# Two float32r products instead of one float32 product for the four gate rows

## The chip, the cores and the metric

The kernel runs on one core of a Trainium2 chip. The core has five engines that work side by side and are tied together by semaphores: TensorE (PE, matrix products; PEld is its weight load), VectorE (DVE), ScalarE (ACT), GpSimd (POOL) and SyncE (SP, which here only issues DMAs). The metric is the device time of one launch in microseconds. The kernel before has a median of 1128.47 us over 3 runs (1128.34 to 1129.39).

## The reference, cut to what matters

One decoder block over 1024 tokens of width 1024, all in float32. A vector of modulations is made from the conditioning vector `c`, and its six parts of 1024 numbers shift, scale and gate the two sub-layers:

```python
cond = jax.nn.silu(c)
mod = cond @ w_ada + b_ada
sh_a, sc_a, gt_a, sh_m, sc_m, gt_m = split(mod, 6)
h = rms_norm(x, g_attn_pre) * (1 + sc_a) + sh_a
...                                    # projection, attention in two kinds of heads, output projection
x = x + gt_a * rms_norm(y, g_attn_post)
h = rms_norm(x, g_mlp_pre) * (1 + sc_m) + sh_m
y = square(relu(h @ w_up)) @ w_down
x = x + gt_m * rms_norm(y, g_mlp_post)
```

The change is about the sums of `cond @ w_ada` for the two gates, `gt_a` and `gt_m`. Each gate has 1024 columns and is made in two groups of 512, so there are four such sums.

## The kernel before, in words

**The modulations.** `w_ada` has 1024 rows; each of the 128 partitions holds 8 of them. The columns behind the first 2048 are worked in eight groups `g` of 512 columns, each in four pieces. `ada_piece` (L1002) loads a piece into a tile `wa_st`, multiplies it by the partition's `cond` and adds it to an accumulator `ada_acc` of 128x512: on POOL for the first 24 pieces (groups 0 to 5, during projection and attention), on DVE for the last 8 (groups 6 and 7, during the MLP). After the fourth piece the 128 partitions have to be summed. For groups 2 to 5 this gives columns, in eight small products. For groups 0, 1, 6 and 7, the gates, the sum is wanted as a row repeated on all partitions: one float32 product with a 128x128 matrix of ones, `f_fin` at L1037, into a PSUM tile `ada_ps`. It stands in the profile as two matmul instructions for each product. The step is planned as `fin`:

```python
T.matmul(b[0][:, :512], ones[:], ada.acc[:, :512], start=True, stop=True)                       # L1037
ef = pe_op("fin", 0.86 if row else 0.45, f_fin, [e], takes=[(r_ps, 1)], gives=[(r_acc or r_adacc, 1)])   # L1041
```

Behind it `f_gl` (L1048, L1049) loads the bias and the gain into a tile `gate_st`, `f_g1` (L1054) adds the PSUM tile to it on DVE and so frees the bank, `f_g2` (L1060, L1062) multiplies, and the row goes to DRAM (`gate_d`), to be read much later as `gate_a` and `gate_m`.

**The rest.** After a start with the loading of `x` and the first modulations, the input projection (`pj`, L875 to L878) runs on PE interleaved with attention: scores `s_ps`, transposes `pt_ps`, probabilities times values `o_ps`, and transposes of values `pv` (L846). Then come the output projection (`y_ps`) and the MLP (`mlp_ps`, L1991 to L1993), where each 512x512 block product is split by sums of blocks into seven products. All large products are made of float32r parts: an operand is cast to a high part on ACT, its low part is made by a subtraction on DVE (or POOL), and three products of parts are added in PSUM. The weights of the projection are split in this way at L549 (ACT) and L554 (DVE or POOL), the probabilities at L1258 and L1262.

**Buffers.** `stage()` (L454) gives a tile of 4 KB a partition: up to the end of the projection one of five (`r_stg`), shared by `wa_st`, `gate_st`, the rotated queries and keys `hl` and the output weights `wo_st` and `wo_hi`; in the MLP one of four that are counted out of a larger pool. `ada_acc` is one buffer (`r_adacc`) in the first part and one of the `stage()` tiles in the MLP. The PSUM bank `x` (`r_x`) is used by `ada_ps`, by `pv`, by every second `o_ps` and, in the MLP, by block products.

**The order.** No engine chooses its order at run time. A planner in the program (`Sched`) goes through all steps before anything is emitted: each step has an engine, an estimated duration, the steps it depends on, buffers that it takes and gives, and a priority. It keeps a clock for each engine, always takes the step that can start earliest by its estimates, and writes the instructions in that order. PE's steps are in named streams, and `prefer()` (L2153) says which stream goes first; `fin` is preferred only 1.0 us after its inputs are due (`SURE`, L143). Loads of priority 15 to 24 are put off by 3 us (`SLACK`, L145). On the chip each engine runs its written order and waits by semaphores. So a step with other durations, or other buffers, can change the order of all steps that are planned after it.

Of the kernel before, what the change touches and what calls it, by code (L numbers as in the profile page):

```python
# [10 lines left out]
F32 = mybir.dt.float32  # L11
F32R = mybir.dt.float32r
# [3 lines left out]
ALU = mybir.AluOpType  # L16
# [3 lines left out]
P = 128  # L20
# [157 lines left out]
class Sched:  # L178
# [21 lines left out]
    def op(self, eng, dur, emit, deps=(), **kw):  # L200

        o = self.step(dur, emit, deps, **kw)
        o.alts = None
        if isinstance(eng, str):
            self.queue[eng].append(o)
        else:
            o.alts = dict(zip(eng, zip(dur, emit)))
            for e in eng:
                self.queue[e].append(o)
        return o.ev  # L210

    def pe_op(self, stream, dur, emit, deps=(), **kw):
        o = self.step(dur, emit, deps, **kw)
        o.alts = None
        self.pe.setdefault(stream, []).append(o)
        return o.ev
# [116 lines left out]
def t_as(n):  # L333
    return 0.2 + 0.00083 * n


def t_dv(n):
    return 0.066 + 0.00104 * n
# [19 lines left out]
def hybrid_block(ctx: ExitStack, tc: tile.TileContext, x, positions, w_ada, b_ada, g_attn_post, w_in, w_out,  # L358
# [3 lines left out]
    V, A, G, T = nc.vector, nc.scalar, nc.gpsimd, nc.tensor  # L362
# [3 lines left out]
    op, pe_op = sc.op, sc.pe_op  # L366
# [9 lines left out]
    const = ctx.enter_context(tc.tile_pool(name="const", bufs=1))  # L376
# [7 lines left out]
    def ring_r(name):  # L384

        return ph2.right.tile([P, 1024], F32, name=name, tag="right")
# [7 lines left out]
    r_stg, r_w, r_wst, r_hl = Res(5), Res(WR), Res(WS), Res(0)  # L394
# [10 lines left out]
    inv_f = head[:, CW_F:CW_F + 8]  # L405
    scl = [head[:, CW_SCL + i:CW_SCL + i + 1] for i in range(2)]
    ones = const.tile([P, P], F32, name="ones")
    nhalf = const.tile([P, KC], F32, name="nhalf")
    cond = const.tile([P, KC], F32, name="cond")
    bb = const.tile([P, KC, 2], F32, name="bb")  # L410
# [43 lines left out]
    def stage(name):  # L454
        if st.stgp is None:
            return ring_r(name)
        return st.stgp.tile([P, 1024], F32, name=name, tag="stg")

    def load(emit, nbytes, deps=(), takes=(), prio=5, gives=(), after=None, n=1):
        return op("SP", nbytes / (345e3 if prio > -500 else 370e3), emit, deps, takes=takes, prio=prio, gives=gives, after=after, n=n)  # L460
# [30 lines left out]
    r_wa, r_acc = Res(NWA), Res(2)  # L491
# [84 lines left out]
    def f_init():  # L576
        V.memset(ones[:], 1.0)
        V.tensor_copy(ones_r[:].rearrange("p (a b) -> p a b", b=P), ones[:].unsqueeze(1).to_broadcast([P, 4, P]))
        V.memset(nhalf[:], -0.5)
    e_init = op("DVE", 0.4, f_init, prio=0)  # L580
    e = op("ACT", 0.1, lambda: A.activation(cond[:], c_raw, AF.Exp, scale=-1.0), [e_c], prio=0)

# [31 lines left out]
    e = op("DVE", 4.2, f_turns, [e_pos, e_c], prio=1)  # L614

    def f_sin():
# [5 lines left out]
                prio=1)  # L622
# [89 lines left out]
    def tables(groups, place, r_place, r_bank, bank, deps):  # L712
# [30 lines left out]
       prio=8)  # L743
# [253 lines left out]
    ada = Tok()  # L997
    ada.i, ada.acc, ada.e, ada.raw, ada.gate = 0, None, Ev(0.0), {}, {}
    e_mod = {}
    r_adacc = Res(1)  # L1000

    def ada_piece(i, eng, accp, psum, r_ps, r_acc=None):  # L1002
        g, jp = divmod(i, 4)
        col = 2 * D + g * 512

        def f_load():
            ada.raw[i] = stage("wa_st")
            nc.sync.dma_start(ada.raw[i][:].rearrange("p (j n) -> p j n", j=2),
                              ada_view[:, 2 * jp:2 * jp + 2, col:col + 512])
        el = load(f_load, 524288, takes=[(r_stg, 1)], prio=20)  # L1010

        def f_acc():
            wa = ada.raw.pop(i)[:].rearrange("p (j n) -> p j n", j=2)
            if jp == 0:
                ada.acc = accp()
            for j in range(2):
                cj = cond[:, 2 * jp + j:2 * jp + j + 1]
                if jp == 0 and j == 0:
                    eng.tensor_scalar(ada.acc[:, :512], wa[:, 0], cj, 1.0, ALU.mult, ALU.mult)
                elif eng is V:  # L1020
                    V.scalar_tensor_tensor(ada.acc[:, :512], wa[:, j], cj, ada.acc[:, :512], ALU.mult, ALU.add)
                else:
                    G.tensor_scalar(wa[:, j], wa[:, j], cj, 1.0, ALU.mult, ALU.mult)
                    G.tensor_tensor(ada.acc[:, :512], ada.acc[:, :512], wa[:, j], ALU.add)  # L1024
        e = op("DVE" if eng is V else "POOL", 1.2 if eng is V else 4.1, f_acc,
               [el, ada.e], takes=[(r_acc or r_adacc, 1)] if jp == 0 else [], gives=[(r_stg, 1)], prio=9)
        ada.e = e
        if jp < 3:
            return
        b = []  # L1030
        row = g in (0, 1, 6, 7)
        n0 = (g % 2) * 512

        def f_fin():
            b.append(psum())
            if row:
                T.matmul(b[0][:, :512], ones[:], ada.acc[:, :512], start=True, stop=True)  # L1037
            else:
                for k in range(4):
                    T.matmul(b[0][:, k:k + 1], ada.acc[:, k * P:(k + 1) * P], ones[:, 0:1], start=True, stop=True)  # L1040
        ef = pe_op("fin", 0.86 if row else 0.45, f_fin, [e], takes=[(r_ps, 1)],  # L1041
                   gives=[(r_acc or r_adacc, 1)])
        if row:
            gate, gp = (gate_d[0], g_attn_post) if g < 2 else (gate_d[1], g_mlp_post)

            def f_gl():
                ada.gate[g] = t = stage("gate_st")
                nc.sync.dma_start(t[:, 0:512], b_ada[0:1, col:col + 512].to_broadcast([P, 512]))  # L1048
                nc.sync.dma_start(t[:, 512:1024], gp[0:1, n0:n0 + 512].to_broadcast([P, 512]))  # L1049
            eg = load(f_gl, 524288, [e], takes=[(r_stg, 1)], prio=19)  # L1050

            def f_g1():
                t = ada.gate[g]
                V.tensor_tensor(t[:, 0:512], b[0][:, :512], t[:, 0:512], ALU.add)  # L1054
            e1 = op("DVE", t_dv(512), f_g1, [ef, eg], gives=[(r_ps, 1)], prio=4)

            def f_g2():
                t = ada.gate[g]
                if g < 2:
                    V.tensor_tensor(t[:, 0:512], t[:, 0:512], t[:, 512:1024], ALU.mult)  # L1060
                else:
                    V.scalar_tensor_tensor(t[:, 0:512], t[:, 0:512], D ** 0.5, t[:, 512:1024], ALU.mult, ALU.mult)  # L1062
            e2 = op("DVE", t_dv(512), f_g2, [e1], prio=4)
            e_mod[g] = load(lambda: nc.sync.dma_start(gate[:, n0:n0 + 512], ada.gate[g][:, 0:512]), 262144, [e2],
                            gives=[(r_stg, 1)], prio=18)
        else:
            k0 = n0 // P

            def f_c():
                if g < 4:  # L1070
                    V.tensor_tensor(s_m[:, k0:k0 + 4], b[0][:, 0:4], cols[:, 40 + k0:44 + k0], ALU.add)
                else:
                    V.tensor_tensor(g_m[:, k0:k0 + 4], b[0][:, 0:4], b1m[:, k0:k0 + 4], ALU.add)
                    V.tensor_tensor(g_m[:, k0:k0 + 4], g_m[:, k0:k0 + 4], cols[:, 16 + k0:20 + k0], ALU.mult)
            e_mod[g] = op("DVE", 0.15, f_c, [ef], gives=[(r_ps, 1)], prio=4)

    def feed_ada():
        if st.d > 1.0 + ada.i * 4.1 / NADA and ada.i < NADA:
            ada_piece(ada.i, G, lambda: adp.tile([P, 512], F32, name="ada_acc", tag="ada_acc", bufs=1), lambda: px.tile([P, 512], F32, name="ada_ps", tag="x"), r_x)
            ada.i += 1  # L1080
        return ada.i == NADA
# [1052 lines left out]
    def feed_ada2():  # L2134
        if ada.i < 32:
            if ada.i >= NADA and ml.begun > 8 + 2 * (ada.i - NADA):
                ada_piece(ada.i, V, lambda: stage("ada_acc"),
                          lambda: px.tile([P, 512], F32, name="ada_ps", tag="x"), r_x, r_stg)
                ada.i += 1
            return False  # L2140

        def f_gate():
            ml.gate = ring_r("gate_m")
            nc.sync.dma_start(ml.gate[:], gate_d[1][:])
        ml.e_gate = load(f_gate, 524288, [e_mod[6], e_mod[7]], takes=[(r_h2, 1)], prio=17)
        return True
# [32 lines left out]
```

## Time and profile before

| what | value |
|---|---|
| median of 3 runs | 1128.47 us (1128.34 to 1129.39) |
| time of the profiled execution | 1129.15 us |
| its span, first to last instruction | 1127.1 us |
| PE busy in the span | 1107.0 us |
| DVE, ACT, POOL busy | 817.2, 636.8, 255.4 us |
| mean granted TensorE clock | 0.996 |
| starts of the four gate products (L1037) | 117.8, 158.4, 663.9 and 813.7 us |

The span is the profiled time less 2.05 us of start and end. Busy time of PE includes the pipeline of a matmul, so two that overlap count once; the distance between starts is the better price of one.

### The profile page before, as it was taken

The page shows a single profiled execution, that of the slowest core. Times are in us where ns is not written, and L with a number is a line of the kernel's source. Part 1 is how long each engine was busy: PE and PEld are TensorE (multiplying, and loading weights), DVE is VectorE, ACT ScalarE, POOL GpSimd, SP SyncE. Part 2 cuts the span into 40 slices and gives each one's busy share as a digit, 9 for nine tenths or more (in the row PEclk, how much of TensorE's full clock was granted, in tenths as well). Part 3 has the DMA queues.
Part 4 walks back from the last instruction along what each step waited for, and adds up shares of the span by engine and source line. Part 5 has one row for each costly group of instructions (what it writes and reads, how often), then busy time and mean ns, then how long its engine had stood idle before and what let it go on. Part 6 is the DMA issues. An engine that isn't in the chain of part 4 may idle for free.

```text
span 1127.1 us, 15613 instructions
## 1 busy us (share of the span) xinstructions
PE 1107.0 (98%) x5417; PEld 920.9 (82%) x5417; DVE 817.2 (73%) x1379; ACT 636.8 (56%) x1111; POOL 255.4 (23%) x336
## 2 busy tenths in 40 slices
PE   8999999999999999999999999999999999999997
PEld 6788888888888788788888888888888888888885
DVE  7968767666686576579889564798743996537998
ACT  8769767455665576677575334653145632246542
POOL 2447777567751131110000000000000000000003
PEclk9999999999999999999999999999999999999999
DMA  9564665554513642565861268711578112584104
GB/s 349 177 215 132 196 225 194 178 173 153 197 43 146 232 147 80 203 235 213 321 242 38 76 233 310 249 52 42 186 252 318 38 56 95 199 307 165 38 19 150
DMA packets 93215, 193.69 MB, mean 172 GB/s; under 512 B 8656, under 2 KB 31312, under 8 KB 93136
## 3 DMA queue, kind: packets, MB, share of 16 engines
q1 hardware_dynamic: 93136, 192.69, 49.2%
q8 instruction: 43, 0.70, 0.3%
q14 instruction: 36, 0.29, 0.1%
HBM read 141.28 MB, written 32.51 MB: 154 GB/s over the span
## 4 chain that ended last, share of the span: by engine, by line
PE 77%; ACT 7%; DVE 6%; DMA 3%; issue 3%; POOL 3%; SPq 1%; POOLq 0%; DVEq 0%; ACTq 0%
PE mlp_ps L1992 17%; PE mlp_ps L1991 17%; PE mlp_ps L1993 17%; PE pj L875 3%; PE pj L878 3%; PE pj L876 3%; PE s_ps L1139 3%; PE o_ps L1274 2%; PE y_ps L1545 2%; PE y_ps L1547 2%; PE y_ps L1546 1%; PE pt_ps L1244 1%; ACT p_sb L1214 1%; PE pt_ps L1247 1%; DMA o_sb<-o_dram 1%
## 5 line engine op out<-in xcount | busy, mean ns | idle before, releaser
L1991 PE MATMUL mlp_ps<-hw 128*128 128x512 f32 x896 | 349.6, 390 | 0.0
L1993 PE MATMUL mlp_ps<-hw 128*128 128x512 f32 x896 | 348.6, 389 | 0.0
L1992 PE MATMUL mlp_ps<-hw 128*128 128x512 f32 x896 | 348.6, 389 | 0.0
L1991 PEld LDWEIGHTS mlp_ps<-hw 128*128 128x128 f32 x896 | 168.2, 188 | 35.8 <-issue 0.5
L1992 PEld LDWEIGHTS mlp_ps<-hw 128*128 128x128 f32 x896 | 168.2, 188 | 35.2 <-issue 0.5
L1993 PEld LDWEIGHTS mlp_ps<-hw 128*128 128x128 f32 x896 | 168.2, 188 | 34.9
L1755 DVE TENSOR_TENSOR hw<-w,hw 128x1024 fp32r<-128x1024 f32 x96 | 114.6, 1219 | 95.2 <-ACT hw L1748 93.2
L1748 ACT CAST hw<-w 128x1024 fp32r<-128x1024 f32 x96 | 97.6, 1048 | 130.0 <-PE mlp_ps L1993 97.5
L2101 POOL TENSOR_TENSOR st<-st,nhalf 128x1 f32<-128x1 f32 x8 | 8.0, 1011 | 592.6 <-DVE st L2099 592.6
L875 PE MATMUL pj<-hw,w_hl 128*128 128x512 f32 x240 | 101.8, 424 | 0.0
L878 PE MATMUL pj<-hw,w_hl 128*128 128x512 f32 x240 | 94.7, 394 | 0.0
L876 PE MATMUL pj<-hw,w_hl 128*128 128x512 f32 x240 | 94.3, 393 | 0.0
L1262 DVE TENSOR_TENSOR ph<-pt_ps,ph 128x512 fp32r<-128x512 f32 (+1 forms) x110 | 68.2, 647 | 24.7 <-ACT ph L1258 24.5
L1748 ACT CAST hw<-u 128x1024 fp32r<-128x1024 f32 x48 | 48.7, 1052 | 64.6 <-PE mlp_ps L1993 64.6
L1258 ACT CAST ph<-pt_ps 128x512 fp32r<-128x512 f32 (+1 forms) x110 | 57.3, 557 | 24.1 <-PE pt_ps L1247 20.3
L1755 DVE TENSOR_TENSOR hw<-u,hw 128x1024 fp32r<-128x1024 f32 x48 | 57.0, 1218 | 18.2 <-ACT hw L1748 18.2
L1165 ACT ACTIVATE p_sb<-p_sb,mn 128x128 f32<-128x128 f32 (+3 forms) x64 | 49.7, 777 | 35.1 <-DVE mn L1158 32.2
L1170 POOL TENSOR_SCALAR p_sb<-p_sb,den 128x128 f32<-128x128 f32 (+3 forms) x64 | 49.0, 771 | 74.1 <-DVE den L1168 66.3
L2049 DVE TENSOR_TENSOR yacc<-yacc,mlp_ps 128x512 f32<-128x512 f32 x96 | 62.1, 681 | 3.3 <-PE mlp_ps L1993 3.3
L1024 POOL TENSOR_TENSOR ada_acc<-ada_acc,wa_st 128x512 f32<-128x512 f32 x42 | 55.8, 1328 | 3.5
L1545 PE MATMUL y_ps<-hw,oh 128*128 128x512 f32 x128 | 52.6, 411 | 0.9 <-DVE mn L1158 0.4
L878 PEld LDWEIGHTS pj<-hw,w_hl 128*128 128x128 f32 x240 | 45.1, 188 | 10.3
(207 smaller groups left out, 1994.1 us busy)
## 6 DMA issues: line engine op xcount, KB each, us to landing
hw<-s_dram SPq DMA_DIRECT2D x84, 512.0 KB, 4.3
wa_st<-in_w_ada SPq DMA_DIRECT2D x32, 512.0 KB, 4.3
w<-in_w_up SPq DMA_DIRECT2D x32, 512.0 KB, 5.5
w<-in_w_down SPq DMA_DIRECT2D x32, 512.0 KB, 6.8
s_dram<-hw SPq DMA_DIRECT2D x28, 512.0 KB, 3.2
qt<-hl SPq DMA_DIRECT2D x40, 256.0 KB, 2.6
w_st<-in_w_in SPq DMA_DIRECT2D x36, 256.0 KB, 3.1
x_sb<-in_x SPq DMA_DIRECT2D x16, 512.0 KB, 5.6
```

The source lines that it names most:

```text
L875: T.matmul(ps, w[:, 0, n], h[0], start=(k == 0), stop=False)
L876: T.matmul(ps, w[:, 1, n], h[0], start=False, stop=False)
L878: T.matmul(ps, w[:, 0, n], h[1], start=False, stop=(k == KC - 1))
L1258: A.copy(b["ph"][:, 0, :w], b["pt"][:, :w])
L1262: V.tensor_tensor(b["ph"][:, 1, :w], b["pt"][:, :w], b["ph"][:, 0, :w].bitcast(F32), ALU.subtract)
L1545: T.matmul(ps[:], b["oh"][:, k], wh[:, c0:c0 + 512], start=(k == 4 * m), stop=False)
L1748: A.copy(out[j][0], flat(src[j]))
L1755: V.tensor_tensor(out[j][1], flat(src[j]), out[j][0].bitcast(F32), ALU.subtract)
L1991: T.matmul(ps[m][:], sh, mh, start=starts and k == 0, stop=False, **kw)
L1992: T.matmul(ps[m][:], sh, ml_, start=False, stop=False, **kw)
L1993: T.matmul(ps[m][:], sl, mh, start=False, stop=k == 3, **kw)
L2049: e = op("DVE", t_dv(512), lambda: V.tensor_tensor(y(), y(), ps[m][:], ALU.add), [e, ml.e_y[tb, n]], gives=gives, prio=1)
```

## The change

The accumulated row sums of the four gate groups are split into a high float32r part (a copy on ACT) and a low float32r part (the difference, on DVE), both in a new tile `acc_hl` from `stage()`; two float32r products with a float32r matrix of ones (`ones_h`, made once at the start on DVE) add up in the PSUM tile. The accumulator is given back after the difference, not after the product; the load of `gate_st` now depends, in the planner, on the difference; and the product is planned with 0.46 in place of 0.86 us. Groups 2 to 5 stay as they are.

```diff
@@ constants
+    ones_h = const.tile([P, P], F32R, name="ones_h")
@@ f_init
         V.memset(nhalf[:], -0.5)
+        V.tensor_copy(ones_h[:], ones[:])
@@ ada_piece
+        hl = []
+
         def f_fin():
             b.append(psum())
             if row:
-                T.matmul(b[0][:, :512], ones[:], ada.acc[:, :512], start=True, stop=True)
+                for i in range(2):
+                    T.matmul(b[0][:, :512], ones_h[:], hl[0][:, i], start=(i == 0), stop=(i == 1))
             else:
...
-        ef = pe_op("fin", 0.86 if row else 0.45, f_fin, [e], takes=[(r_ps, 1)],
-                   gives=[(r_acc or r_adacc, 1)])
+        if row:
+            acc = []
+
+            def f_ah():
+                acc.append(ada.acc)
+                hl.append(stage("acc_hl")[:].rearrange("p (s n) -> p s n", s=2).bitcast(F32R))
+                A.copy(hl[0][:, 0], acc[0][:, :512])
+
+            def f_al(eng):
+                return lambda: eng.tensor_tensor(hl[0][:, 1], acc[0][:, :512], hl[0][:, 0].bitcast(F32), ALU.subtract)
+            e = op("ACT", t_as(512), f_ah, [e], takes=[(r_stg, 1)], prio=4)
+            ada.e = e
+            e = op("DVE", t_dv(512), f_al(V), [e], gives=[(r_acc or r_adacc, 1)], prio=4)
+        ef = pe_op("fin", 0.46 if row else 0.45, f_fin, [e], takes=[(r_ps, 1)],
+                   gives=[(r_stg if row else r_acc or r_adacc, 1)])
```

## The prediction

> **What bounds the kernel now.** I read the page's busy shares and its chain first, then busy time by stretch, then the four products one by one.
>
> ```profile
> PE 1107.0 (98%) x5417; PEld 920.9 (82%) x5417; DVE 817.2 (73%) x1379; ACT 636.8 (56%) x1111; POOL 255.4 (23%) x336
> PE 77%; ACT 7%; DVE 6%; DMA 3%; issue 3%; POOL 3%; SPq 1%; POOLq 0%; DVEq 0%; ACTq 0%
> ```
>
> ```profile
> core 0: us, PE busy (x) PEld busy (x) DVE busy (x) ACT busy (x) POOL busy (x), PEclk, DMA share, GB/s
> 0.00:110.00 110.00, 103.67 (x549) 85.54 (x550) 85.59 (x209) 88.15 (x181) 54.82 (x93) 1.00 0.66 223
> 110.00:180.00 70.00, 68.61 (x369) 55.96 (x368) 48.33 (x127) 50.26 (x133) 53.67 (x80) 1.00 0.66 213
> 180.00:376.00 196.00, 195.20 (x1140) 167.72 (x1139) 138.41 (x361) 116.69 (x249) 110.58 (x123) 1.00 0.43 147
> 376.00:500.00 124.00, 120.99 (x635) 101.19 (x634) 81.07 (x169) 77.43 (x130) 23.17 (x29) 0.99 0.51 171
> 500.00:1088.00 588.00, 587.78 (x2597) 485.33 (x2596) 431.20 (x461) 291.63 (x394) 2.56 (x3) 1.00 0.48 170
> 1088.00:1127.10 39.10, 30.72 (x136) 25.11 (x134) 32.63 (x56) 12.61 (x29) 10.59 (x10) 0.94 0.29 108
> ```
>
> PE is the bound from about 110 us to 1088 us, and in the MLP (500 to 1088 us) it idles 0.22 us in 588. Between 110 and 500 us its idle time is 1.39 + 0.80 + 3.01 = 5.2 us. So whatever shortens PE's own work behind 110 us shortens the span, if the order around it stays as good. The chain of waits, in order of time, has these pieces at and around the products:
>
> ```profile
> 117.69 0.23 PE pj L878
> 117.92 0.86 PE ada_ps L1037 x2
> 118.78 0.39 PE s_ps L1194 x4
> ...
> 160.96 1.29 POOL ada_acc L1024
> ...
> 169.72 0.69 DVE gate_st L1054
> 170.46 0.66 PE pv L846 x4
> ...
> 663.80 0.23 PE mlp_ps L1993
> 664.04 0.86 PE ada_ps L1037 x2
> 664.90 0.23 PE mlp_ps L1991
> ...
> 813.87 0.86 PE ada_ps L1037 x2
> 814.72 0.23 PE mlp_ps L1991
> ```
>
> The reader sees that three of the four products lie on the chain with PE's work directly before and behind them, each for 0.86 us. Around the second one, at 158 us, the chain leaves PE and goes over ACT, POOL's accumulation and the gate's addition on DVE. The second group's last addition on POOL, and PE's instructions behind it:
>
> ```profile
> 154.81 2.13 POOL L1024 TENSOR_TENSOR ada_acc<-ada_acc,wa_st 128x512 f32<-128x512 f32 x1
> ...
> 158.39 1.02 PE L1037 MATMUL ada_ps<-ada_acc,ones 128*128 128x512 f32 x2
> 158.85 0.80 PE L875 MATMUL pj<-hw,w_hl 128*128 128x512 f32 x1
> 159.48 0.40 PE L876 MATMUL pj<-hw,w_hl 128*128 128x512 f32 x1
> 159.72 0.39 PE L878 MATMUL pj<-hw,w_hl 128*128 128x512 f32 x1
> ```
>
> From the start of the pair to that of the second matmul behind it are 1.09 us; less one step of 0.24 (159.48 to 159.72) the pair takes 0.85 us here too.
>
> **The change part by part.**
>
> *The products.* A float32r product of the same shape takes 0.23 us of PE (the rows of the chain beside the pair), so two take 0.46, and 0.40 us goes at each of four places: 1.6 us. The two at 664 and 814 us stand in a stretch where PE never waits, so 0.8 us is as good as sure; at 118 us the product is on the chain as well; at 158 us PE is 98% busy, but something else is on the chain, so that share is 0 to 0.4. I take 1.6, with 1.2 as the low end. The Trainium skill, FP8 and Floating Point Precision, section TensorE Precision Notes, says that a true FP32 product makes four passes through the array; by it the pair would be 0.92 and the saving 1.8 us, and the row (0.86, in two instructions) decides for 1.6.
>
> *The two parts.* Each sum gains a copy on ACT and a subtraction on DVE of 128x512. The same forms stand in the trace for the projection's weights:
>
> ```profile
> L549 ACT CAST w_hl<-w_st x36: 602/620/642, 15.8 to 318.4; 128x512 fp32r<-128x512 f32 x36
> L554 POOL TENSOR_TENSOR w_hl<-w_st,w_hl x21: 1277/1292/2104, 52.2 to 311.3; 128x512 fp32r<-128x512 f32 x21
> L554 DVE TENSOR_TENSOR w_hl<-w_st,w_hl x15: 674/694/1712, 16.7 to 319.1; 128x512 fp32r<-128x512 f32 x15
> ```
>
> So 0.62 + 0.69 = 1.31 us more before the product can start, and in all 2.5 us more ACT and 2.8 us more DVE. What hides it: neither engine is the bound, and the planner asks that `fin` be 1.0 us past due before it is preferred, with other streams running meanwhile. In the MLP:
>
> ```profile
> 666.32 1.05 ACT L1748 CAST hw<-w 128x1024 fp32r<-128x1024 f32 x1 [4.80 <-PE mlp_ps L1993]
> 666.09 0.69 DVE L1054 TENSOR_TENSOR gate_st<-ada_ps,gate_st 128x512 f32<-128x512 f32 x1 [2.76 <-PE mlp_ps L1992]
> ...
> 748.64 1.53 DVE L1021 SCALAR_TENSOR_TENSOR ada_acc<-wa_st,cond,ada_acc 128x512 f32<-128x512 f32 x2
> ```
>
> Between 661.5 and 666 us both engines have idle time (4.80 and 2.76 us). The fourth sum is ready at 750.2, its product comes at 813.9: 64 us of cover. At 118 and 158 us:
>
> ```profile
> 115.41 0.59 ACT L1258 CAST ph<-pt_ps 128x512 fp32r<-128x512 f32 x1 [2.12 <-PE pt_ps L1251]
> 118.07 0.68 DVE L1326 TENSOR_TENSOR ot<-o_ps,otmp 64x512 f32<-64x512 f32 x1 [0.70 <-ACT otmp L1321]
> 160.23 0.51 ACT L1214 ACTIVATE p_sb<-p_sb,mn 128x257 f32<-128x257 f32 x1 [1.41 <-DVE mn L1209]
> 166.96 0.68 DVE L772 TENSOR_TENSOR hl<-pj,tab 64x512 f32<-64x512 f32 x1 [4.43 <-PE pj L878]
> ```
>
> ACT has 2.12 and 1.41 us idle nearby; DVE only 0.70 at the first place and 4.43 at the second. Without that cover, what is queued behind the subtraction (the low part of the probabilities at L1262, or the row maxima at L1209) comes 0.69 us later, and PE's `o_ps` or ACT's exponentials wait for it; with projection matmuls to run in between I cost this at nothing and keep 2 x 0.69 = 1.4 us as an end.
>
> The DVE row has a spread: 0.69 as a rule, 1.71 when it fell beside a POOL addition, and POOL's own 1.29 became 2.10. The Trainium skill, SBUF — State Buffer, section SBUF: two separate sides, has a rule for it: VectorE with two SBUF inputs and GpSimd exclude each other from a shared port for a whole instruction. The maxima of both rows agree with it; it speaks against the change at the first two sums, where POOL is 77% busy (53.67 of 70 us).
>
> *Buffers and queues.* The accumulator comes back behind the subtraction; POOL may go on with the next group without waiting for PE. At 158 us the product started 1.45 us behind the end of the last addition (156.94); with 1.31 us and waits in two queues the accumulator comes back at about the same time, so nothing either way. The copy takes one of the five stage tiles until the product is done. In the planner the loads of `gate_st` come behind the subtraction, 1.3 us and more later, and pass on SP behind whatever has become ready by then:
>
> ```profile
> 154.09 0.59 SPq L1008 DMA_DIRECT2D wa_st<-in_w_ada  x1
> 161.07 0.80 SPq L1048 DMA_DIRECT2D gate_st<-in_b_ada  x1
> ...
> DMA to landing us min/median/max: 4.4/5.3/7.6
> ```
>
> The addition at 169.72 stands behind the rotation of a projection tile that starts at 166.96, so a load that is issued 1.3 us later, at 162.4, is still there by then with the median landing of 5.3 us, and by 170.0 with the longest of 7.6 us: 0 to 0.3 us for `pv`, which stands behind the addition. I take nothing.
>
> *The start.* One more DVE copy of 128x128 into `ones_h`:
>
> ```profile
> 1.02 0.43 DVE L578 CAST ones_r<-ones 128x512 fp32r<-128x512 f32 x1
> 2.38 0.17 DVE L597 CAST posf<-posi 128x8 f32<-128x8 int32 x1 [0.92 <-DMA posi<-in_positions]
> ```
>
> A quarter of the copied 0.43 us is 0.1 us and fits the 0.92 us in which DVE waits for a DMA: nothing.
>
> *The plan.* The steps up to the end of the first accumulation (about 110 us) are planned as before. Behind it every start in the planner shifts, and the order of any later steps may come out otherwise. The trace of before can't price this: below, a part of the 5.2 us of PE's idle time may go; above, a stall of PE for one or two buffers of some us each may come. I take 0, because PE has projection matmuls or MLP products ready nearly all the time, and the balance of 0.22 us idle in the MLP cannot get much worse by a few displaced steps.
>
> *The sum.* Against the profiled execution: 1129.15 - 1.6 = 1127.55 us, with a span of 1125.5. That execution is 0.68 us above the median, so the median comes to 1128.47 - 1.6 = 1126.9 us, 0.14% less. A change of 0.2% (2.3 us) is about what a measurement of this kernel can tell from none.
>
> **The rivals.**
>
> *The new plan has fewer stalls.* For it: the chain at 155 to 170 us runs over ACT, POOL and the gate's addition, so small shifts there count, and 5.2 us of idle PE is there to be had. Against it: the MLP, half of the time, has none. With half of the 5.2 us gone besides: 1126.9 - 2.6 = 1124.3 us.
>
> *A stage tile is missing (slower).* The place is the second sum. `wa_st`, loaded at 154.09, is in use until POOL's addition ends at 162.25, 8.2 us; the rotation at 166.96 needs a stage tile as well, and one more is now held from the copy to the product. If the rotation has to wait, its PSUM bank stays taken and the projection stops. Half of those 8.2 us, as attention fills the other half: 1126.9 + 4.1 = 1131.0 us. Against it: the rotation now waits 4.43 us for PE and not for a buffer. It decides from 1.6 us of lost PE time on, and can be measured as slower from 3.9 us on.
>
> *POOL and DVE shut each other out.* Two subtractions of 1.7 in place of 0.7 us that PE has to wait for: 1126.9 + 2.0 = 1128.9 us. For it: the maxima above. Against it: PE has other work.
>
> *The two products save nothing.* If loading the ones twice or the change of type cost as much as the pair: 1128.5 us. Against it stand 0.23 us for every float32r product, each with a weight load of its own.
>
> **How the numbers follow.** The saving as summed, with plans neutral within 1.5 us: 0.44. Fewer stalls: 0.21. Stage tile: 0.26. Shared port: 0.05. Nothing saved: 0.04. Below 1126.2 (faster by 0.2%) lies a third of the first case, 0.14, so faster has 0.14 + 0.21 = 0.35; slower has the 0.26 of the stage tile; the rest, 0.39, is within 0.2%. The range goes from 1123.0, half of a 2.6 us gain beyond the second case, to 1131.0, the price of the third, and leaves out some 0.07 below and 0.12 above. The likeliest case alone is 1125.4 to 1128.4.
>
> **What would show it.** L1037 or its successor as eight float32r matmuls of 0.39 us, 0.46 us for each pair on the chain; MLP idle time of PE still below 1 us; the four copies at 0.62 and the subtractions at 0.69, or 1.7 beside POOL; between 110 and 500 us PE idle time near 5.2 us. The prediction is wrong if that idle time changes by more than 2 us, if the rotation (L772) or `pv` wait for a stage tile or the gate's addition, or if the tail behind 1088 us is arranged otherwise.

## The result and the profile after

The changed kernel takes 1130.49 us in the median of 10 runs (1129.33 to 1132.71), beside 1128.21 us for the kernel before in 10 runs (1126.23 to 1129.39). The ratio is 1.0023, with a 95% interval of 1.0014 to 1.0033: slower by 2.6 us (1.6 to 3.7), where 1.6 us less was forecast. Every ratio below compares runs of one chip and leaves disturbed ones out, so it isn't exactly the quotient of the medians.

The profiled execution of the changed kernel is its fastest, 1129.33 us. It is only 0.2 us above the profiled execution before, which had lost more than 1 us to a lower clock at 384 to 390 us (last section); the price of the change is that of the medians, not of these two profiles. From its page, the span, the busy shares and the shares of the chain of waits:

```profile
span 1127.6 us, 15623 instructions
PE 1104.9 (98%) x5417; PEld 920.0 (82%) x5417; DVE 822.1 (73%) x1388; ACT 640.9 (57%) x1118; POOL 246.7 (22%) x329
PE 71%; DVE 7%; ACT 3%; issue 2%; DMA 2%; SPq 1%; POOL 1%; POOLq 0%; DVEq 0%; ACTq 0%
```

PE has 2.1 us less busy time (1107.0 before) and yet the span is not shorter: the time is in its gaps. Busy time by the stretches used in the prediction (columns: from:to, length, then busy us and count for PE, PEld, DVE, ACT, POOL, then granted clock, DMA share, GB/s):

```profile
110.00:180.00 70.00, 65.85 (x363) 54.45 (x362) 50.74 (x138) 54.02 (x142) 44.82 (x75) 1.00 0.57 175
180.00:376.00 196.00, 194.52 (x1127) 166.65 (x1127) 138.26 (x355) 113.92 (x240) 111.23 (x122) 1.00 0.47 157
376.00:500.00 124.00, 120.64 (x644) 100.74 (x644) 80.74 (x169) 77.16 (x130) 23.13 (x29) 1.00 0.52 176
500.00:1088.00 588.00, 587.84 (x2600) 486.04 (x2599) 433.10 (x463) 293.84 (x398) 2.56 (x3) 1.00 0.48 170
```

PE's idle time between 110 and 180 us has grown from 1.39 to 4.15 us, from 180 to 376 us from 0.80 to 1.48, and in the MLP it stays at nothing (0.22 and 0.16). So the loss lies around the first two sums. The other two did what was forecast; the chain of waits in the MLP:

```profile
666.42 0.23 PE mlp_ps L2011
666.65 0.46 PE ada_ps L1042 x2
667.11 0.23 PE mlp_ps L2009
...
814.49 0.23 PE mlp_ps L2011
814.72 0.46 PE ada_ps L1042 x2
815.18 0.23 PE mlp_ps L2009
```

Each pair takes 0.46 in place of 0.86 us. Setting the start of each MLP matmul against that of the same matmul in the profile before, the lag falls by 0.39 us at the third sum and by 0.40 us at the fourth, and by nothing between. Between 110 and 225 us, in the same comparison, the changed kernel falls back from 0.58 us ahead to 1.65 us behind. (The 0.58 us are not the change's: e7 below, which splits nothing, is 0.61 us ahead at the same place.)

Where this happens is seen in the timeline between 158 and 170 us (start, duration, engine and line; in brackets the idle time before and what ended it):

```profile
158.42 1.29 POOL L1026 TENSOR_TENSOR ada_acc<-ada_acc,wa_st 128x512 f32<-128x512 f32 x1
...
160.20 0.62 ACT L1052 CAST acc_hl<-ada_acc 128x512 fp32r<-128x512 f32 x1
163.15 0.68 DVE L1055 TENSOR_TENSOR acc_hl<-ada_acc,acc_hl 128x512 fp32r<-128x512 f32 x1
163.99 0.69 POOL L1021 TENSOR_SCALAR ada_acc<-wa_st,cond 128x512 f32<-128x512 f32 x1 [3.69 <-ACT p_sb L1232]
165.44 1.29 POOL L1026 TENSOR_TENSOR ada_acc<-ada_acc,wa_st 128x512 f32<-128x512 f32 x1
166.76 1.15 ACT L1385 ACTIVATE wo_hi<-wo_st,head 128x1024 fp32r<-128x1024 f32 x1 [3.69 <-POOL ada_acc L1026]
168.31 0.56 ACT L1276 CAST ph<-pt_ps 128x512 fp32r<-128x512 f32 x1
168.92 0.49 PE L1304 MATMUL o_ps<-ph,v_hl 128*128 128x512 f32 x1 [2.19 <-ACT ph L1276]
169.88 0.50 PE L1304 MATMUL o_ps<-ph,v_hl 128*128 128x512 f32 x1 [0.46 <-DVE ph L1280]
```

Read it downwards. The second sum's last addition on POOL ends at 159.71, its copy on ACT at 160.82. Its subtraction stands on DVE behind four row maxima and an addition and starts 2.33 us later. It is now the last reader of the only accumulator, so POOL, idle for 3.69 us, begins the third group at 163.99. (The bracket names ACT's `p_sb`, but its last row ends at 163.08 and the subtraction at 163.83; that POOL waits for the accumulator is shown by e4 below, where a second one takes the wait away.) POOL's addition ends at 166.73 and gives back a stage tile (`wa_st`). ACT has been idle for 3.69 us for that tile, because the next step in its queue, `wo_hi`, writes to one; the fifth tile is held by `acc_hl`. Behind `wo_hi` stand the casts of the probabilities, and PE waits for those: 2.19 + 0.46 = 2.65 us. In the kernel before, the same two steps stood like this:

```profile
152.44 1.14 ACT L1367 ACTIVATE wo_hi<-wo_st,head 128x1024 fp32r<-128x1024 f32 x1
...
159.51 0.70 POOL L1019 TENSOR_SCALAR ada_acc<-wa_st,cond 128x512 f32<-128x512 f32 x1
```

`wo_hi` came ahead of the hand-off, and the third group began 4.48 us earlier. The hand-off makes 4.10 of these 4.48 us: in e4, where the order up to here is the changed kernel's too, the third group begins at 159.89. The other 0.38 us come with the new order. The Trainium skill, PSUM — Partial Sum Buffer, section Engine vs sequencer instructions, says that the queues of ScalarE, VectorE and GpSimd are strict FIFO. The trace agrees: the transposes that the cast at 168.31 reads were issued on PE at 163.61, and yet ACT did nothing for 3.69 us.

### The profile page after: what moved, and what is told of

It reads as the page before. It is cut to its first block, busy times and chain, and to the rows that moved or that the text cites. A ratio compares the mean times of both kernels' runs of the same rounds, so it can differ in the third digit from the quotient of the medians.

```text
span 1127.6 us, 15623 instructions
## 1 busy us (share of the span) xinstructions
PE 1104.9 (98%) x5417; PEld 920.0 (82%) x5417; DVE 822.1 (73%) x1388; ACT 640.9 (57%) x1118; POOL 246.7 (22%) x329
## 4 chain that ended last, share of the span: by engine, by line
PE 71%; DVE 7%; ACT 3%; issue 2%; DMA 2%; SPq 1%; POOL 1%; POOLq 0%; DVEq 0%; ACTq 0%
PE mlp_ps L2010 16%; PE mlp_ps L2009 16%; PE mlp_ps L2011 16%; PE s_ps L1157 3%; PE pj L877 3%; PE pj L880 3%; PE pj L878 3%; PE y_ps L1563 2%; PE y_ps L1565 1%; PE y_ps L1564 1%; PE o_ps L1292 1%; PE pt_ps L1262 1%; DMA o_sb<-o_dram 1%; DVE hw L1773 1%; PE pt_ps L1265 1%
```

## The experiments

Three theories were set against each other. *The hand-off*: the loss is the hole at 166 to 170 us, made by one link of accumulator, POOL, stage tile and `wo_hi`; freeing any link takes it away. *The operations*: a copy and a subtraction cost PE's time wherever they stand. *The order*: the planner's new order loses time as such.

**Only the MLP's two sums split (e1).**

```diff
+        parts = g in (6, 7)
...
-            if row:
+            if parts:
                 for i in range(2):
                     T.matmul(b[0][:, :512], ones_h[:], hl[0][:, i], start=(i == 0), stop=(i == 1))
+            elif row:
+                T.matmul(b[0][:, :512], ones[:], ada.acc[:, :512], start=True, stop=True)
...                                    # copy and subtraction for these two alone; 0.86 stays for the others
```

> Only the two sums of the MLP (groups 6 and 7) are split; those of groups 0 and 1 stay one float32 product. Theory A (the loss of 2.3 us comes from the new order behind the first two sums): the written order up to the MLP is that of the kernel before, so 0.8 us faster than before (ratio 0.9993), with PE steps of 0.46 us for each pair at 664 and 814 us. Theory B (the added copies, subtractions or the float32r matrix of ones cost time wherever they stand): slower than before, by about 1.1 us if the loss is shared evenly.

Measured: 1126.59 us beside 1127.42, ratio 0.9989 (0.9980 to 0.9998), so 1.2 us less (0.2 to 2.3); in the profile PE's lag falls by 0.39 us at each of the two sums. The products pay where PE never waits, and the operations are free there: the theory of the operations falls for this half.

**Only the attention's two sums split (e2).** The same edit with `g in (0, 1)`.

> Only the two sums of groups 0 and 1 are split; groups 6 and 7 stay as before. Theory A: the whole loss is here, and the MLP's gain of 0.8 us is missing: 2.3 + 0.8 = 3.1 us slower than before (ratio 1.0027), with PE idle time near 4 us between 110 and 180 us as in the changed kernel. Theory B: half of the loss, about 1.1 us slower.

Measured: 1130.93 us, ratio 1.0028 (1.0018 to 1.0039). The stretch with the hole, in busy time:

```profile
160.00:170.00 10.00, 7.34 (x38) 5.58 (x36) 5.63 (x15) 6.21 (x16) 2.96 (x6) 1.00 0.63 225
```

PE is busy for 7.34 of 10 us, exactly as in the full change: the whole loss, and the same hole, belong to this half.

**All four split, every queue in the order of before (e3).** The parts are made directly ahead of the product in a tile that isn't a stage tile, and the product stays planned with 0.86 us:

```diff
...                                    # ones_h; f_ah, f_al: each runs once, into a tile of the pool `early`
+        if row:
+            op("DVE", 0.0, f_al, [op("ACT", 0.0, f_ah, [e], prio=4)], prio=4)
...
-                T.matmul(b[0][:, :512], ones[:], ada.acc[:, :512], start=True, stop=True)
+                f_al()
+                for i in range(2):
+                    T.matmul(b[0][:, :512], ones_h[:], hl[0][:, i], start=(i == 0), stop=(i == 1))
```

> All four sums are split, but every engine's order is that of the kernel before, with the copy, the subtraction and the two products put in where the plan of before has room: they take no time and no stage tile in the planner (a tile of another pool holds the two parts), and the product is still planned with 0.86 us. Theory A: no loss from order; 1.6 us off for the products, and up to 2 us on where the product at 158 us waits on PE for the subtraction: 1.6 us faster to 0.4 us slower than before. Theory B: as slow as the changed kernel, 2.3 us over before.

Measured: 1128.47 us, ratio 1.0007 (0.9998 to 1.0016), worse than expected. Here the product stands where it stood, and PE waits for the parts, as the timeline shows:

```profile
117.66 0.50 PE L1058 MATMUL ada_ps<-acc_hl,ones_h 128*128 128x512 f32 x1 [0.35 <-DVE acc_hl L1048]
...
158.77 0.49 PE L1058 MATMUL ada_ps<-acc_hl,ones_h 128*128 128x512 f32 x1 [0.85 <-ACT acc_hl L1042]
159.50 0.50 PE L1058 MATMUL ada_ps<-acc_hl,ones_h 128*128 128x512 f32 x1 [0.23 <-DVE acc_hl L1048]
```

0.35 + 0.85 + 0.23 = 1.43 us: nearly the 1.4 us that the prediction kept as an end for uncovered parts. So the parts are not free at the first two sums unless the product is put later, and the planner's order, which puts the first product at 149.3 in place of 117.8 us and the second at 179.5 in place of 158.4, has its use too. Without the hole the loss is within what can be told from none.

**The full change with two accumulators (e4).**

```diff
-    r_adacc = Res(1)
+    r_adacc = Res(2)
...
-            ada_piece(ada.i, G, lambda: adp.tile([P, 512], F32, name="ada_acc", tag="ada_acc", bufs=1), ...
+            ada_piece(ada.i, G, lambda: adp.tile([P, 512], F32, name="ada_acc", tag="ada_acc", bufs=2), ...
```

> The changed kernel with two accumulator buffers in the first part in place of one. The order on PE and SP is the same as in the changed kernel, and on the others two or three instructions differ. Theory A1 (POOL's first step of the next group waits for the subtraction, so that the output weights' copy on ACT waits for a stage tile, and PE stands idle near 167 us): the idle time of 2.66 us between 160 and 170 us goes, and the kernel comes to 0.4 us under before, 2.7 us under the changed kernel (ratio to before 0.9997). Theory A2 (the order as a whole is worse, and this wait is only where it shows): still 2 us over before (1.0020).

Measured: 1126.54 us, ratio 0.9990 (0.9981 to 0.9999), so 1.1 us less than before and 3.7 us less than the change. PE's and SP's orders are those of the change, with a few steps changing places on the other engines. Its busy time in the stretch, and its timeline:

```profile
160.00:170.00 10.00, 10.00 (x55) 8.41 (x54) 8.15 (x23) 8.51 (x22) 6.48 (x10) 1.00 0.78 261
```

```profile
159.89 0.69 POOL L1021 TENSOR_SCALAR ada_acc<-wa_st,cond 128x512 f32<-128x512 f32 x1
161.34 1.31 POOL L1026 TENSOR_TENSOR ada_acc<-ada_acc,wa_st 128x512 f32<-128x512 f32 x1
162.67 1.15 ACT L1385 ACTIVATE wo_hi<-wo_st,head 128x1024 fp32r<-128x1024 f32 x1
```

POOL begins 4.10 us earlier than in the change, `wo_hi` runs 4.09 us earlier and without a wait, and the hole is gone. The copy and the subtraction are all still there, so the theory of the operations falls here too.

**The other links: `wo_hi` (e5) or the first two sums' parts (e6) in a tile of their own.** All five orders are those of the change.

```diff
-                hi.append(stage("wo_hi"))
+                hi.append(early.tile([P, 1024], F32, name="wo_hi", tag="early"))          # e5
...
-                hl.append(stage("acc_hl")[:]...
+                hl.append((early.tile(...) if g < 2 else stage("acc_hl"))[:]...           # e6
```

> The changed kernel, every engine's order unchanged, one accumulator; only the high part of the output weights (wo_hi) lies in a tile of another pool instead of a stage tile, so that its copy on ACT does not wait for POOL. Theory A1 with the stage tile as the link between POOL and PE: POOL still waits 3.7 us for the subtraction, but ACT no longer waits and the idle time of 2.66 us between 160 and 170 us goes: 2.7 us under the changed kernel, 0.4 us under before (ratio 0.9997). If POOL's wait itself is what costs (its later work comes late), no more than 1 us is won and the kernel stays at 1.0015 or above.

> The changed kernel, every engine's order unchanged, one accumulator; only the two parts of the first two sums lie in a tile of another pool, while the planner still counts a stage tile for them. With five stage tiles for the rest, the copy of the output weights finds a free one and does not wait for POOL. Theory A1 (the fifth stage tile is missing): the same gain as with wo_hi apart, 2.7 us under the changed kernel (ratio to before 0.9997). If the stage tiles are not short: as the changed kernel (1.0023).

Measured: 1126.98 and 1127.32 us, both ratios 1.0002 (0.9993 to 1.0011): 2.4 us less than the change. The two stretches in e5, and the timeline of e6:

```profile
160.00:170.00 10.00, 10.00 (x55) 8.38 (x54) 8.82 (x24) 9.38 (x24) 5.76 (x9) 1.00 0.47 138
170.00:200.00 30.00, 28.39 (x155) 23.55 (x154) 22.64 (x51) 18.62 (x39) 20.23 (x21) 1.00 0.79 258
```

```profile
163.09 1.14 ACT L1385 ACTIVATE wo_hi<-wo_st,head 128x1024 fp32r<-128x1024 f32 x1
163.26 0.68 DVE L1055 TENSOR_TENSOR acc_hl<-ada_acc,acc_hl 128x512 fp32r<-128x512 f32 x1
164.10 0.69 POOL L1021 TENSOR_SCALAR ada_acc<-wa_st,cond 128x512 f32<-128x512 f32 x1 [3.70 <-ACT p_sb L1232]
```

With identical orders the hole goes as soon as `wo_hi` needn't wait for the tile, though POOL still starts its third group as late as in the change. So it was the stage tile, not POOL's delay as such, that reached PE. As these two runs keep every order, their 2.4 us are the strictest measure of that link. The cure is only partial: PE idles 1.61 us between 170 and 200 us in e5, where e4 has 0.43. What of this comes from POOL's remaining delay and what from other steps was not separated.

**Two controls on the second accumulator (e7, e9).** e7 gives the kernel before two accumulators; e9 gives e4 the edit of e5 as well. In each pair all orders are the same.

> The kernel before with two accumulators in the first part and nothing else; every engine's order is that of before. In before POOL's first step of the second next group starts at 159.5 us, right behind its own work, so I expect no wait to be removed: the same time as before (ratio 1.0000, within 0.4 us). If a second accumulator is worth 0.9 us by itself, the gain of the changed kernel with two accumulators over before is not the change's.

> The change with two accumulators and, besides, wo_hi in a tile of its own; every engine's order is that of the run with two accumulators alone. If the hand-off through the accumulator and the stage tile is all that the change lost between 110 and 200 us, a second cure at the same place adds nothing: 0.9990 again, within 0.001, PE idle below 0.3 us between 160 and 170 us. If links with the stage tiles cost PE elsewhere in the attention too, it gains another 1 us or more: 0.9981 or less.

Measured: e7 1126.57 us, ratio 0.9996 (0.9987 to 1.0005), e9 1126.02 us, ratio 0.9988 (0.9980 to 0.9997). The second buffer gains nothing measurable by itself, and a second cure at the same place adds nothing that can be told from none: the two are one loss.

**The order alone (e8).** The kernel before, nothing split, with one number of the plan changed:

```diff
-        ef = pe_op("fin", 0.86 if row else 0.45, f_fin, [e], takes=[(r_ps, 1)],
+        ef = pe_op("fin", 0.46 if row else 0.45, f_fin, [e], takes=[(r_ps, 1)],
```

> The kernel before with only the planned duration of the four products lowered from 0.86 to 0.46 us; the instructions are those of before, and some 40 rows of PE's order change places. Theory A (order matters, but only where it makes an engine wait) leaves the sign open: within 1 us of before (0.9991 to 1.0009). Theory A2 (any new order behind 110 us costs some 2 us): about 1.0020.

Measured: 1131.58 us, ratio 1.0042 (1.0030 to 1.0055). Both expectations were missed: an order in which some 40 of PE's rows change places costs 4.7 us, more than the change itself. The timeline shows one hole:

```profile
133.86 1.26 POOL L1024 TENSOR_TENSOR ada_acc<-ada_acc,wa_st 128x512 f32<-128x512 f32 x1
135.15 0.59 ACT L789 ACTIVATE hl<-pj 64x512 fp32r<-64x512 f32 x1 [3.36 <-POOL ada_acc L1024]
...
136.38 0.68 DVE L1326 TENSOR_TENSOR ot<-o_ps,otmp 64x512 f32<-64x512 f32 x1
...
137.21 0.63 PE L731 MATMUL ptab<-head,rows 128*128 128x128 f32 x4 [3.08 <-DVE ot L1326]
```

By the trace it is the same link (no run takes the link away from this order): a step of ACT that writes to a stage tile (`hl`, here) is written behind a POOL addition that gives one back, everything behind it on ACT waits, and PE idles for 3.08 us. Behind it the granted clock was 0.82 from 135 to 140 us and 0.83 from 140 to 145, by estimate 0.18 x 5 + 0.17 x 5 = 1.75 us more. No part of the split is needed for it.

**The change with the old planned duration (e10), with two accumulators besides (e11), and with each sum bound to its accumulator (e12).**

```diff
-        ef = pe_op("fin", 0.46 if row else 0.45, f_fin, ...                    # e10, e11, e12
+        ef = pe_op("fin", 0.86 if row else 0.45, f_fin, ...
...
+            own.append(ada.acc)                                                # e12, in f_acc
-                    T.matmul(b[0][:, k:k + 1], ada.acc[:, k * P:(k + 1) * P], ...
+                    T.matmul(b[0][:, k:k + 1], own[0][:, k * P:(k + 1) * P], ...
```

> The change with the pair's planned duration put back to 0.86 (it takes 0.46): the same work, PE's rows in another order in some 60 places behind the second sum. Theory of the hand-off: the hole depends on what DVE and ACT have queued ahead of the subtraction and of the copy wo_hi, so another order moves the time by anything from -3 to +3 us; with the hole kept, 1.0023; without it, 0.9990 to 1.0005. Rival, that the split as such costs about 3 us at the attention's sums in any order: 1.0023 whatever PE's order is.

> The run before (planned 0.86) with two accumulators. If the second accumulator takes away what made the time depend on the order, this comes to 0.9990 +- 0.001, as two accumulators did with the other order, whatever the run with one shows. If the gain of the two accumulators was that one order's luck, it can come out anywhere between 0.998 and 1.002.

> The run before this one (two accumulators, planned 0.86) with each group's sum bound to its own accumulator: there, PE's one-column products of the third group (L1045) were issued behind the next group's first step, read that group's accumulator instead of their own, and waited 2.6 us for POOL's addition into it. Nothing else changes. If that wait was the whole loss, the time falls from 1.0046 to 1.0023 or less by the 2.6 us, and to 0.9990 if the second accumulator makes the time independent of the order. If PE's other holes of that order (1.9 us for the gate's addition and those before 170 us) stay, it remains between 1.0015 and 1.003.

Measured: 1131.72 us, ratio 1.0032 (1.0020 to 1.0044), for e10; 1133.08, 1.0046 (1.0034 to 1.0058), for e11; 1129.08, 1.0013 (1.0004 to 1.0022), for e12. e10 keeps the hole, and its time fits the theory of the hand-off and, just as well, its rival (the split costs some 3 us in any order); what speaks against the rival are e4, e5 and e6, which keep the split and lose the hole. e11 misses what was expected of it. In e11 the third group's column products read the fourth group's accumulator, since the step names the current one when it is written out; so its modulations are wrong, and its time says only what such a wait costs: the work has the same size, but PE waits 2.6 us for an addition that it doesn't need. e12 binds each sum to its own accumulator and is 3.7 us faster. The timeline of e10, where PE's order is another but the link is the same:

```profile
164.69 0.69 DVE L1055 TENSOR_TENSOR acc_hl<-ada_acc,acc_hl 128x512 fp32r<-128x512 f32 x1
165.53 0.69 POOL L1021 TENSOR_SCALAR ada_acc<-wa_st,cond 128x512 f32<-128x512 f32 x1 [4.65 <-ACT p_sb L1232]
166.98 1.29 POOL L1026 TENSOR_TENSOR ada_acc<-ada_acc,wa_st 128x512 f32<-128x512 f32 x1
168.30 1.15 ACT L1385 ACTIVATE wo_hi<-wo_st,head 128x1024 fp32r<-128x1024 f32 x1 [3.66 <-POOL ada_acc L1026]
169.48 1.28 DVE L1389 SCALAR_TENSOR_TENSOR wo_st<-wo_st,head,wo_hi 128x1024 fp32r<-128x1024 f32 x1 [4.10 <-ACT wo_hi L1385]
...
171.49 0.73 PE L1042 MATMUL ada_ps<-acc_hl,ones_h 128*128 128x512 f32 x2 [2.49 <-DVE v_hl L859]
```

The same three waits, 4.65, 3.66 and 4.10 us, end this time in the product itself, which waits for a PSUM bank that DVE empties behind `wo_st`. With two accumulators that chain is gone, and the longest wait left in e12 is another one of that order, at the gate's addition:

```profile
179.80 0.68 DVE L1074 TENSOR_TENSOR gate_st<-ada_ps,gate_st 128x512 f32<-128x512 f32 x1
...
180.62 1.17 PE L1306 MATMUL o_ps<-ph,v_hl 128*128 128x512 f32 x4 [1.91 <-DVE gate_st L1074]
```

So a second accumulator is worth 3.7 us in one order (e4 beside the change, with a few steps of the other engines in other places). In the other order e12 is 2.1 us below e10, but this isn't the buffer alone: up to 182.7 us PE's order is the same in both, and there the same matmuls gain 4.3 us between 166 and 178; behind it the planner, given a second buffer, orders PE otherwise, and about half of the gain is lost again. The second accumulator doesn't make the time independent of the order, as the expectation had it: with it in place, 0.46 and 0.86 as the planned duration still differ by 2.6 us (0.9990 and 1.0013).

e4 and e9 beat both kernels, by 1.1 and 1.4 us against before. Against before with two accumulators (e7, 0.9996) the difference isn't clear of the noise.

## Why the prediction was wrong

It was forecast to be 0.14% faster and is 0.23% slower, inside the range, on the other side of no change: a gap of 0.37% or 4.2 us.

- **The products** were right: 0.46 us a pair, 0.8 us in the MLP (e1). The four passes of the Trainium skill, FP8 and Floating Point Precision, section TensorE Precision Notes, at the prediction's estimate of 0.23 us each, would have made it 0.46 us a pair less; the 0.39 and 0.40 us of the MLP don't agree with that estimate and do with the row of 0.86 us.
- **The two parts** were right in length, as the rows of the tile `acc_hl` in the changed kernel say (shortest, median and longest in ns, then first and last start):

```profile
L1052 ACT CAST acc_hl<-ada_acc x4: 622/622/624, 112.6 to 751.1; 128x512 fp32r<-128x512 f32 x4
L1055 DVE TENSOR_TENSOR acc_hl<-ada_acc,acc_hl x4: 681/685/1157, 116.7 to 752.1; 128x512 fp32r<-128x512 f32 x4
```

  Their cost of nothing held in the MLP. At the first two sums nothing held only because the planner put the product later; where it stayed, PE waited 1.43 us (e3), the end that was kept.
- **Buffers and queues** is the step that failed first: "the accumulator comes back at about the same time, so nothing either way". Of the 1.45 us between the last addition and the product it left 1.45 - 1.31 = 0.14 us for the waits in two queues. These took 0.49 us on ACT (159.71 to 160.20) and 2.33 us on DVE, 2.82 us together, and the hand-off put off POOL's next group by 4.10 us (e4). And the sentence did not go on to who waits for POOL: a stage tile, and through it ACT and PE (e4, e5, e6). Taking the link away gives back 3.7 of the 4.2 us (e4), or 2.4 us with every order kept (e5, e6). The load of `gate_st`, 0 to 0.3 us there, caused no wait in the change; in the order of e12 the addition behind it holds PE for 1.91 us.
- **The plan**, "I take 0, because PE has projection matmuls or MLP products ready nearly all the time", failed too. PE's queue is written as well: a product that waits holds the ready ones behind it (2.49 us in e10). Moving `wo_hi` behind the hand-off was the planner's doing, and an order alone can cost 4.7 us (e8).
- **The rival "a stage tile is missing"** came true in its place, the second sum, and in its condition, one more tile held from the copy to the product (160.2 to 179.5 us). The waiting step was not the rotation L772, as it was put, but `wo_hi`, and its cover was gone through the accumulator. Its price of 4.1 us over the forecast meets the 4.2 us measured by luck, as its working (half of 8.2 us) isn't what happened: PE's hole is 2.65 us, and what the clock may do behind it comes on top, below. The condition also came true at the first sum, whose tile is held from 112.6 to 149.7 us: POOL has to wait for a stage tile to hold `rows` (the input of the rotation's tables, L965), and PE then 0.67 us for a table at 134.73. The row of the changed kernel, and that of e6, where the parts lie apart and neither wait is there:

```profile
131.11 0.95 POOL L721 MEMSET rows<- 128x1024 f32 x1 [5.91 <-DMA qt<-hl]
```

```profile
125.40 0.98 POOL L721 MEMSET rows<- 128x1024 f32 x1
```

- **The rivals of fewer stalls and of two products that save nothing** did not come: PE's idle time grew, and each pair in the MLP saves 0.39 or 0.40 us.
- **The start** and **the MLP's cover** held: PE idles 0.16 us in the MLP. Between 110 and 500 us its idle time went from 5.2 to 4.15 + 1.48 + 3.36 = 9.0 us, beyond the 2 us that the prediction named as the mark of being wrong.
- **POOL and DVE shut each other out** was seen once and priced nothing; the timeline of the changed kernel at the first sum:

```profile
116.01 1.30 POOL L783 TENSOR_TENSOR hl<-hl 128x512 fp32r<-128x512 f32 x1 [2.05 <-ACT hl L780]
116.70 1.16 DVE L1055 TENSOR_TENSOR acc_hl<-ada_acc,acc_hl 128x512 fp32r<-128x512 f32 x1
117.27 1.73 POOL L555 TENSOR_TENSOR w_hl<-w_st,w_hl 128x512 fp32r<-128x512 f32 x1
```

  The subtraction took 1.16 in place of 0.68 us, and no wait of PE stands behind it. The Trainium skill, SBUF — State Buffer, section SBUF: two separate sides, has the engine that starts later wait for the whole of the other's instruction; the trace agrees in kind: the subtraction, begun 0.61 us ahead of the end of POOL's, took 0.48 us more, and POOL's next, begun beside it, 0.44 us more than the 1.29 us of its row.

## What to carry to other kernels

When a change makes a new instruction the last reader of a single buffer, follow that buffer to the end: who writes it next, which tile that writer gives back, and which queue stands still for the tile. A step that writes to a shared ring of tiles, queued ahead of urgent work, turns any late release into a stall of everything behind it, so a second buffer at the hand-off, or a tile of its own for that step, can decide more than the operation saved (here 3.7 or 2.4 us against 1.6). In a kernel whose order is planned from estimates, change the estimate alone as a control before a gain or a loss is put down to the operations.

## What the hardware showed besides

A hole of PE can cost more than its length. After the same hole (2.66 us of idle time between 160 and 170 us in both) the next 5 us went as follows, first in e2, then in the changed kernel's profile (columns as above; the granted clock is the third number from the end):

```profile
170.00:175.00 5.00, 5.00 (x20) 4.04 (x20) 3.46 (x10) 3.28 (x10) 1.71 (x4) 0.66 0.37 134
```

```profile
170.00:175.00 5.00, 5.00 (x28) 4.23 (x29) 4.45 (x14) 4.42 (x12) 2.13 (x5) 1.00 0.38 135
```

In e2 the clock was 0.66 and 20 matmuls began in place of 28: by estimate 0.34 x 5 = 1.7 us lost behind the hole (in slices of 1 us the clock is 0.50 from 171 to 173 us). The orders are the same there, and by the starts of the same matmuls e2 falls 1.6 us behind the changed kernel at this place. The profile before shows the same at another place, between attention and output projection, after two gaps of 0.44 and 0.53 us of PE:

```profile
384.00:390.00 6.00, 5.47 (x22) 4.41 (x22) 3.42 (x8) 1.95 (x3) 0.00 (x0) 0.72 0.51 168
```

This is 0.28 x 6 = 1.7 us again by estimate. In e1, whose order is the same there and whose clock is 1.00, the same matmuls gain 1.3 us against before between 370 and 395 us. It fits that this execution, at 1129.15 us, was above most of its kind. The mean clock of an execution goes with its time: of the changed kernel's ten, the fastest had 0.998 and the other nine 0.994 to 0.997. So the changed kernel's median is 1.2 us above its profiled execution probably because most of its executions lose such a stretch behind the hole; the executions without a profile show only their mean clock, so this isn't shown. The Trainium skill, TensorE: Matmul & The Clock Gate, section What's actually happening, says that the gate halves the clock after a free-running window of some 3.4 us without activity; that the same hole is followed by the lower clock in one execution and not in another agrees with a free-running window, while the gaps ahead of the two rows (2.19 and 0.46 us in e2, 0.44 and 0.53 us before) are all shorter than it.
